# Hybrid trunk on one core: the output projection's second half in pieces, and another order of the final norm

## The chip, the cores and the metric

One core of one Trainium2 chip. The metric is the device time of one execution in microseconds, median of several runs. The core has five engines with a queue of instructions each: TensorE (PE, with its weight loads listed as PEld), VectorE (DVE), ScalarE (ACT), GpSimd (POOL) and SyncE (SP), which here only issues DMAs. Matmuls write accumulators in PSUM; a tile there that takes one bank is 128 partitions by 512 fp32 numbers.

## The reference

A trunk of two layers on x (512 positions by 1024 features, fp32), each a token mixer and a dense MLP with residual adds, and a last norm:

```python
def rmsnorm(x, g):
    y = xf * lax.rsqrt(jnp.mean(xf * xf, axis=-1, keepdims=True) + RMS_EPS)
    return (y * g).astype(x.dtype)

h = x
for layer in range(DEPTH):                       # 2
    hn = rmsnorm(h, norm_mix[layer])
    if layer % N_MIXERS == 0:                    # layer 0: 16 heads of 64, softmax over a band
        mix = chunked_band_attention(hn, attn_w_qkv[j], attn_w_o[j], attn_rel_bias[j])
    else:                                        # layer 1: gated linear recurrence
        mix = rglru_block(hn, ...)
    h = h + mix
    h = h + sq_relu_mlp(rmsnorm(h, norm_mlp[layer]), mlp_w1[layer], mlp_w2[layer])
return rmsnorm(h, norm_final)
```

The attention adds a bias to the scores by relative position, takes the softmax over each position's band of keys, weighs v by it, and multiplies the heads' outputs by w_o.

## The kernel before, in words

All activations are held transposed, features on the partitions: `hT[m]` (named h or x in the trace) is the residual of feature tile m, 128 features by 512 positions, eight tiles in all. Each fp32 product is made of two parts of each factor, a rounded high one (`hnH`, `wh`, `kh`, `pH`, `oH`) and the rest (`hnL`, `wl`, `kl`, `pL`, `oL`): `mm3` (L201 to 204) issues three matmuls, high by high, high by low and low by high. Weights come in blocks of 512 KB (`wr`, buffer pool of three, issued by SP); ACT makes `wh` of a block (L132) and DVE `wl` (L135).

**Attention.** Heads go in pairs p (heads 2p and 2p+1). For a pair the projection gives q and k; `k_out` scales k (`tk`, DVE), ACT makes `kh`, DVE `kl`, and SP copies each to the other half of the partitions by a DMA (L319 and L320), since a score matmul uses both halves. `score(h)` makes the scores of four blocks t of 128 positions, with 128(t+1) keys each, in three PSUM tiles: s0 holds t = 0 and 1, s1 t = 2, s2 t = 3; for each t first with kl, then with kh. DVE adds the bias and takes the maximum (L387), ACT the exponential, DVE scales. `turn(h)` transposes the result on PE (x, L414); ACT makes `pH` (L418) and DVE `pL` (L419) of it. `weigh(h)` multiplies by v into `oa` (L429 with pL, L430 with pH); ACT and DVE bring the halves together into `o`, and for a pair `oH` and `oL` are made. The output projection (`wo_steps`) adds, per feature tile, the products of four pairs' o with w_o: woA over pairs 0 to 3, woB over pairs 4 to 7.

The loop over i issues `score(i)`, `turn(i-1)` and `weigh(i-2)`, and between them `fill` takes pieces from a queue written out by hand (projections q, k, v, then woA and woB), as many as a credit allows, and only those whose condition holds: ("w", 15) means that `weigh(15)` has been issued. A scheduler then reorders the instructions of each engine by its own estimate of when each can start. PSUM has two pools of four banks: "mm" for projections, oa and wo, "at" for scores, transposes, sums and rows.

**Last norm.** In the last MLP the down projection of layer 1 is done in two halves of the positions, h = 0 and 1, 256 positions each. For each feature tile DVE adds the residual (L739); ACT squares it and DVE adds the square to `nf0acc` or `nf1acc` (L237, L238); in half 1 the square of the last tile is made on DVE and kept apart (`nf1sq`, L234). `sums` (L261) adds over the partitions by matmuls with ones, per 128 positions, into `nf1ss`; ACT takes the square root, DVE the reciprocal (`rt`, L265 and L266). `rstd` (L274) spreads `rt` over the partitions by a product with the identity, `nf1row`. Then DVE multiplies each tile by gain and row (`nf1o`, L731), and SP issues one DMA of 256 KB for every two tiles (L732). `finish` of half 0 stands in the order behind tile 1 of half 1.

At the start, `warm` multiplies ones by ones ten times.

Of the kernel before, what the change touches and what calls it, by code (L numbers as in the profile page):

```python
# [10 lines left out]
F32 = mybir.dt.float32  # L11
F32R = mybir.dt.float32r
AF = mybir.ActivationFunctionType
ALU = mybir.AluOpType

P = 128
# [24 lines left out]
def trunk(ctx: ExitStack, tc: tile.TileContext, xT, cols, win, wqkv, wo, rwin, rga, rgx, rwo, w1, w2, out):  # L41
# [10 lines left out]
    def mmp(name):  # L52
        return ps.tile([P, T], F32, name=name, tag="mm")

    def atp(name):
        return ps.tile([P, T], F32, name=name, tag="at")
# [144 lines left out]
    def mm3(acc, WH, WL, XH, XL, start, stop):  # L201
        PE.matmul(acc, WH, XH, start=start, stop=False)  # L202
        PE.matmul(acc, WH, XL, start=False, stop=False)  # L203
        PE.matmul(acc, WL, XH, start=False, stop=stop)  # L204
# [8 lines left out]

    LO, HI = slice(0, U), slice(U, T)


    class Norm:
        def __init__(self, name, gain, c0=0, n=T, late=False, flat=False):
            self.name, self.gain, self.acc, self.last, self.c, self.n = name, gain, None, None, slice(c0, c0 + n), n
            self.late, self.flat = late, flat  # L220
# [5 lines left out]

        def square(self, k, apart=False):
            if self.acc is None:
                self.acc = wk.tile([P, T], F32, name=f"{self.name}acc", tag="nacc")[:, : self.n]
                S.activation(self.acc, hT[k][:, self.c], AF.Square)  # L230
            else:
                sq = wk.tile([P, T], F32, name=f"{self.name}sq{k}", tag="nsq", bufs=2)[:, : self.n]
                if apart:
                    V.tensor_mul(sq, hT[k][:, self.c], hT[k][:, self.c])  # L234
                    self.last = sq
                    return
                S.activation(sq, hT[k][:, self.c], AF.Square)  # L237
                V.tensor_add(self.acc, self.acc, sq)  # L238

        def feed(self, k):  # L240
# [8 lines left out]
        def sums(self):  # L249
            nt = self.n // P  # L250
            ss = atp(f"{self.name}ss")
            if self.flat:
                PE.matmul(ss, ones, self.acc, start=True, stop=True)
                self.r = wk.tile([P, T], F32, name=f"{self.name}r", tag="nr")
                S.activation(self.r, ss, AF.Sqrt, bias=epsb, scale=1.0 / D)
                V.reciprocal(self.r, self.r)
                return
            parts = [self.acc] if self.last is None else [self.acc, self.last]
            for t in range(nt):
                for n, part in enumerate(parts):  # L260
                    PE.matmul(  # L261
                        ss[:, 2 * t : 2 * t + 2], part[:, t * P : (t + 1) * P], ones[:, 0:2],
                        start=n == 0, stop=n == len(parts) - 1,
                    )
            S.activation(rt[:, :nt], ss[:, 0 : 2 * nt : 2], AF.Sqrt, bias=epsb, scale=1.0 / D)  # L265
            V.reciprocal(rt[:, :nt], rt[:, :nt])  # L266

        def rstd(self):
            if self.flat:
                return self.r  # L270
            nt = self.n // P
            row = atp(f"{self.name}row")
            for t in range(nt):
                PE.matmul(row[:, t * P : (t + 1) * P], rt[:, t : t + 1].to_broadcast([P, P]), ident, start=True, stop=True)  # L274
            if self.last is not None:
                return row[:, : self.n]
            r = wk.tile([P, T], F32, name=f"{self.name}r", tag="nr")[:, : self.n]
            S.copy(r, row[:, : self.n])
            return r

# [3 lines left out]
    with ExitStack() as actx:  # L284
# [69 lines left out]

        def wo_steps(pairs, ncols, last):
            for u in range(D // ncols):
                WH, WL = want(1)
                for i in range(ncols // P):
                    m = u * (ncols // P) + i
                    acc = mmp(f"wo{pairs[0]}{m}")  # L360
                    c = slice(i * P, (i + 1) * P)
                    for n, p in enumerate(pairs):
                        mm3(acc, WH(n, c), WL(n, c), *oHL[p], n == 0, n == len(pairs) - 1)
                        yield 2
                    V.tensor_add(hT[m], acc, hT[m])
                    if last:
                        nm1.feed(m)

# [4 lines left out]
        def score(h):  # L373
# [6 lines left out]
            b = biases[h // 4]  # L380
            for t in range(4):
                n = (t + 1) * P
                PE.matmul(sc[t], q[h][:, t * P : n], kl[:, :n], start=True, stop=False)
                PE.matmul(sc[t], q[h][:, t * P : n], kh[:, :n], start=False, stop=True)
            for t in range(4):
# [58 lines left out]

        warm = atp("warm")
        for i in range(WARM):
            PE.matmul(warm[:, :P], ones, ones, start=True, stop=True)
        accs = [mmp(f"qk0{i}") for i in range(4)]
# [40 lines left out]

        def wo_(name, pairs, ncols, last):  # L490
            return [(name, wo_steps(pairs, ncols, last), ("w", 2 * pairs[-1] + 1))]

        queue = vv_(0) + qk(2) + qk(3) + qk(4) + vv_(1) + qk(5) + qk(6) + qk(7)
        queue += wo_("woA", (0, 1, 2, 3), U, False) + wo_("woB", (4, 5, 6, 7), U, True)
        at = {"s": -1, "w": -1}
# [44 lines left out]
    def constants(behind):  # L540
# [26 lines left out]
        V.tensor_add(cbias, cbias, cst[:, C_CB : C_CB + KT])  # L567

    PAIR = (slice(0, P), slice(P, 2 * P))

# [7 lines left out]
    def mlp(ly, norm, nxt, halves):  # L578
        with ExitStack() as mctx:
# [142 lines left out]

            def finish(nf):
                nf.sums()
                rf = nf.rstd()
                for m in range(0, KT, 2):
                    o = sr.tile([P, 1024], F32, name=f"{nf.name}o{m}", tag=("b11", "b21", "b22", "b12")[m // 2])
                    o = o[:, :T].rearrange("p (i c) -> p i c", i=2)
                    for i in range(2):
                        g = cst[:, C_FIN + m + i : C_FIN + m + i + 1]  # L730
                        V.scalar_tensor_tensor(o[:, i], hT[m + i][:, nf.c], g, rf, ALU.mult, ALU.mult)  # L731
                    nc.sync.dma_start(out[m * P : (m + 2) * P, nf.c].rearrange("(k p) c -> p k c", p=P), o)  # L732

            for h, nf in enumerate(norms):
                for m in range(KT):
                    acc = mmp(f"d{ly}7{m}{h}")[:, :U]
                    WH, WL = ws[m // 2]
                    project([acc], [PAIR[m % 2]], WH, WL, [(z[7, k][0][:, nf.c], z[7, k][1][:, nf.c]) for k in range(4)])
                    V.tensor_add(hT[m][:, nf.c], acc, hT[m][:, nf.c])  # L739
                    nf.square(m, h == 1 and m == KT - 1)  # L740
                    if h and m == 1:
                        finish(norms[0])
            finish(norms[1])

# [189 lines left out]
```

## Time and profile before

| | |
|---|---|
| median of the runs | 1082.8 us (1083.53, 1082.6, 1082.8) |
| the profiled execution | 1082.37 us, its span 1080.6 us |
| PE busy | 1069.6 us, 99% of the span |
| DVE, ACT, POOL busy | 863.5, 531.3, 9.0 us |
| DMA | 111.15 MB, mean 103 GB/s |

The span runs from the first to the last event of the engines and queues; the 1.8 us around it belong to the device time too. Busy times are sums of overlapping instructions: a matmul starts before the one ahead of it is through, so that the distance from one start to the next tells how long it holds PE, not its own duration. In the rows, "[0.90 <-DVE pL L419]" behind an instruction means that its engine stood idle for 0.90 us before it, and that DVE's instruction writing pL at line 419 ended that.

### The profile page before, as it was taken

The page shows a single profiled execution, that of the slowest core. Times are in us where ns is not written, and L with a number is a line of the kernel's source. Part 1 is how long each engine was busy: PE and PEld are TensorE (multiplying, and loading weights), DVE is VectorE, ACT ScalarE, POOL GpSimd, SP SyncE. Part 2 cuts the span into 40 slices and gives each one's busy share as a digit, 9 for nine tenths or more (in the row PEclk, how much of TensorE's full clock was granted, in tenths as well). Part 3 has the DMA queues.
Part 4 walks back from the last instruction along what each step waited for, and adds up shares of the span by engine and source line. Part 5 has one row for each costly group of instructions (what it writes and reads, how often), then busy time and mean ns, then how long its engine had stood idle before and what let it go on. Part 6 is the DMA issues. An engine that isn't in the chain of part 4 may idle for free.

```text
span 1080.6 us, 15337 instructions
## 1 busy us (share of the span) xinstructions
PE 1069.6 (99%) x6046; PEld 935.6 (87%) x6046; DVE 863.5 (80%) x1286; ACT 531.3 (49%) x775; POOL 9.0 (1%) x28
## 2 busy tenths in 40 slices
PE   9999999999999999999999999999999999999996
PEld 7888888888899999898988888888889999989896
DVE  6889788879887787776777989879887777787665
ACT  6667567565443343342444688366443343343321
POOL 0010000000000000000000000000000000000000
PEclk9999999999999999999999999999999999999999
DMA  8354253341432323322232222442431432332102
GB/s 275 98 140 134 59 176 98 83 152 59 137 117 79 117 89 107 99 81 96 76 122 77 78 64 73 151 142 68 147 117 59 136 98 79 117 94 83 59 1 79
DMA packets 112919, 111.15 MB, mean 103 GB/s; under 512 B 4176, under 2 KB 106704, under 8 KB 112848
## 3 DMA queue, kind: packets, MB, share of 16 engines
q1 hardware_dynamic: 112560, 109.99, 33.1%
q8 instruction: 47, 0.77, 0.3%
q14 instruction: 24, 0.20, 0.1%
q10 hardware_dynamic: 288, 0.20, 0.1%
HBM read 103.87 MB, written 2.10 MB: 98 GB/s over the span
## 4 chain that ended last, share of the span: by engine, by line
PE 96%; DVE 2%; ACT 1%; DMA 1%; issue 0%; SPq 0%; DVEq 0%; ACTq 0%
PE d L203 11%; PE d L202 11%; PE d L204 11%; PE p L204 9%; PE p L203 9%; PE p L202 9%; PE x L414 1%; PE wo L203 1%; PE wo L202 1%; PE ro L202 1%; PE v L202 1%; PE ro L204 1%; PE v L204 1%; PE wo L204 1%; PE xb L202 1%; PE xb L204 1%
## 5 line engine op out<-in xcount | busy, mean ns | idle before, releaser
L132 ACT CAST wh<-wr 128x1024 fp32r<-128x1024 f32 (+1 forms) x129 | 133.6, 1039 | 201.6 <-PE d L203 88.8
L203 PE MATMUL d<-zL,wh 128*128 128x512 f32 (+1 forms) x544 | 206.3, 379 | 0.0
L202 PE MATMUL d<-zH,wh 128*128 128x512 f32 (+1 forms) x544 | 205.1, 379 | 0.0
L204 PE MATMUL d<-zH,wl 128*128 128x512 f32 (+1 forms) x544 | 204.8, 377 | 0.0
L132 ACT CAST wh<-b 128x1024 fp32r<-128x1024 f32 x98 | 101.3, 1047 | 174.8 <-PE p L203 76.0
L135 DVE TENSOR_TENSOR wl<-wr,wh 128x1024 fp32r<-128x1024 f32 (+1 forms) x130 | 156.2, 1203 | 23.3 <-ACT wh L132 23.1
L135 DVE TENSOR_TENSOR wl<-b,wh 128x1024 fp32r<-128x1024 f32 x98 | 118.7, 1219 | 42.9 <-ACT wh L132 42.8
L204 PE MATMUL p<-tH,wl 128*128 128x256 f32 x448 | 126.8, 283 | 0.0
L203 PE MATMUL p<-tL,wh 128*128 128x256 f32 x448 | 126.8, 283 | 0.0
L202 PE MATMUL p<-tH,wh 128*128 128x256 f32 x448 | 126.6, 282 | 0.0
L204 PEld LDWEIGHTS d<-zH,wl 128*128 128x128 f32 x544 | 102.4, 188 | 19.1
L202 PEld LDWEIGHTS d<-zH,wh 128*128 128x128 f32 x544 | 102.5, 189 | 16.8
L203 PEld LDWEIGHTS d<-zL,wh 128*128 128x128 f32 x544 | 102.7, 189 | 16.3 <-DVE zL L623 0.5
L678 DVE TENSOR_TENSOR h<-d,h 128x512 f32<-128x512 f32 x120 | 82.2, 686 | 38.9 <-PE d L204 38.3
L204 PE MATMUL p<-hnH,wl 128*128 128x256 f32 x336 | 95.1, 283 | 0.0
L203 PE MATMUL p<-hnL,wh 128*128 128x256 f32 x336 | 95.1, 283 | 0.0
L202 PE MATMUL p<-hnH,wh 128*128 128x256 f32 x336 | 94.9, 282 | 0.0
L202 PEld LDWEIGHTS p<-tH,wh 128*128 128x128 f32 x448 | 85.8, 192 | 1.6
L203 PEld LDWEIGHTS p<-tL,wh 128*128 128x128 f32 x448 | 85.8, 192 | 1.6
L204 PEld LDWEIGHTS p<-tH,wl 128*128 128x128 f32 x448 | 85.8, 192 | 0.0
L202 PEld LDWEIGHTS p<-hnH,wh 128*128 128x128 f32 x336 | 64.3, 191 | 1.7
L203 PEld LDWEIGHTS p<-hnL,wh 128*128 128x128 f32 x336 | 64.3, 191 | 1.6
(336 smaller groups left out, 2071.6 us busy)
## 6 DMA issues: line engine op xcount, KB each, us to landing
wr<-in_w SPq DMA_DIRECT2D x72, 512.0 KB, 3.5
b<-in_w SPq DMA_DIRECT2D x56, 512.0 KB, 4.4
wr<-in_wqkv SPq DMA_DIRECT2D x20, 512.0 KB, 4.0
wr<-in_rwin SPq DMA_DIRECT2D x16, 512.0 KB, 3.6
wr<-in_wo SPq DMA_DIRECT2D x8, 512.0 KB, 4.2
wr<-in_rwo SPq DMA_DIRECT2D x8, 512.0 KB, 3.4
x<-in_xT SPq DMA_DIRECT2D x8, 256.0 KB, 4.3
bias<-in_win SPq DMA_DIRECT2D x4, 512.0 KB, 4.5
```

Source lines behind the costliest of these rows:

```text
L132: S.copy(H[:, :n], raw[:, :n])
L135: low = V.tensor_sub(L[:, :n], raw[:, :n], f(H[:, :n]))
L202: PE.matmul(acc, WH, XH, start=start, stop=False)
L203: PE.matmul(acc, WH, XL, start=False, stop=False)
L204: PE.matmul(acc, WL, XH, start=False, stop=stop)
L414: PE.transpose(b[:, c : c + P], pt[:, seg[t] + kt * P : seg[t] + (kt + 1) * P], ident)
L678: V.tensor_add(hT[m], acc, hT[m])
```

## The change

It has three parts.

1. `wo_steps` takes a range of weight blocks. Block 0 of woB is split: `wo_open` multiplies pairs 4, 5 and 6 for its two feature tiles as soon as `weigh(13)` is issued, `wo_close` adds pair 7 after `weigh(15)`; the other blocks follow as before.
2. `score` goes through the blocks t in the order 3 and 2, 0, 1, and for each of these first with kh, then with kl.
3. In the last norm, ACT multiplies each tile by its gain as soon as the tile is there (`scale`, into the output tiles). What is left, the product with the row, is done on DVE for four tiles at once (128x1024) and one DMA of 512 KB. In half 1 the squares of tiles 6 (ACT) and 7 (DVE) are kept apart, the two sums have a bank each and a square root each, five products on ones by ones (`idle`) are written ahead of the last sums and of the row, and the row is made twice: DVE takes the one in PSUM for tiles 0 to 3 and then 4 and 5, ACT copies the other for GpSimd, which does tiles 6 and 7 and whose DMA ACT issues. The outputs of half 1 go in DMAs of 512, 256 and 256 KB.

`warm` is now written with `idle` and takes its bank from the "mm" pool.

```diff
+    PAIR = (slice(0, P), slice(P, 2 * P))
+    def idle(n):
+        bank = mmp("idle")
+        for _ in range(n):
+            PE.matmul(bank[:, :P], ones, ones, start=True, stop=True)
...
-        def square(self, k, apart=False):
+        def square(self, k, apart=None):
             if self.acc is None:
                 self.acc = wk.tile([P, T], F32, name=f"{self.name}acc", tag="nacc")[:, : self.n]
                 S.activation(self.acc, hT[k][:, self.c], AF.Square)
+                self.parts.append(self.acc)
+                return
+            sq = wk.tile([P, T], F32, name=f"{self.name}sq{k}", tag="nsq", bufs=2)[:, : self.n]
+            if apart is V:
+                V.tensor_mul(sq, hT[k][:, self.c], hT[k][:, self.c])
             else:
-                sq = wk.tile([P, T], F32, name=f"{self.name}sq{k}", tag="nsq", bufs=2)[:, : self.n]
-                if apart:
-                    V.tensor_mul(sq, hT[k][:, self.c], hT[k][:, self.c])
-                    self.last = sq
-                    return
                 S.activation(sq, hT[k][:, self.c], AF.Square)
+            if apart is None:
                 V.tensor_add(self.acc, self.acc, sq)
+            else:
+                self.parts.append(sq)
...
-            parts = [self.acc] if self.last is None else [self.acc, self.last]
-            for t in range(nt):
-                for n, part in enumerate(parts):
+            if len(self.parts) > 1:
+                ss = [atp(f"{self.name}ss{t}")[:, 0:2] for t in range(nt)]
+            else:
+                row = atp(f"{self.name}ss")
+                ss = [row[:, 2 * t : 2 * t + 2] for t in range(nt)]
+            for n, part in enumerate(self.parts):
+                if n and n == len(self.parts) - 1:
+                    idle(2)
+                for t in range(nt):
                     PE.matmul(
-                        ss[:, 2 * t : 2 * t + 2], part[:, t * P : (t + 1) * P], ones[:, 0:2],
-                        start=n == 0, stop=n == len(parts) - 1,
+                        ss[t], part[:, t * P : (t + 1) * P], ones[:, 0:2],
+                        start=n == 0, stop=n == len(self.parts) - 1,
                     )
-            S.activation(rt[:, :nt], ss[:, 0 : 2 * nt : 2], AF.Sqrt, bias=epsb, scale=1.0 / D)
+            if len(self.parts) > 1:
+                for t in range(nt):
+                    S.activation(rt[:, t : t + 1], ss[t][:, 0:1], AF.Sqrt, bias=epsb, scale=1.0 / D)
+            else:
+                S.activation(rt[:, :nt], row[:, 0 : 2 * nt : 2], AF.Sqrt, bias=epsb, scale=1.0 / D)
             V.reciprocal(rt[:, :nt], rt[:, :nt])
 
-        def rstd(self):
+        def rstd(self, copies=1):
             if self.flat:
                 return self.r
             nt = self.n // P
-            row = atp(f"{self.name}row")
-            for t in range(nt):
-                PE.matmul(row[:, t * P : (t + 1) * P], rt[:, t : t + 1].to_broadcast([P, P]), ident, start=True, stop=True)
-            if self.last is not None:
-                return row[:, : self.n]
+            rows = [atp(f"{self.name}row{i}") for i in range(copies)]
+            if copies > 1:
+                idle(3)
+            for row in rows:
+                for t in range(nt):
+                    PE.matmul(row[:, t * P : (t + 1) * P], rt[:, t : t + 1].to_broadcast([P, P]), ident, start=True, stop=True)
             r = wk.tile([P, T], F32, name=f"{self.name}r", tag="nr")[:, : self.n]
-            S.copy(r, row[:, : self.n])
-            return r
+            S.copy(r, rows[-1][:, : self.n])
+            return r if copies == 1 else (r, rows[0][:, : self.n])
...
+        open_ = []
+        def wo_tile(m, acc, last):
+            V.tensor_add(hT[m], acc, hT[m])
+            if last:
+                nm1.feed(m)
+        def wo_steps(pairs, us, last):
+            for u in us:
                 WH, WL = want(1)
-                for i in range(ncols // P):
-                    m = u * (ncols // P) + i
-                    acc = mmp(f"wo{pairs[0]}{m}")
-                    c = slice(i * P, (i + 1) * P)
+                for i in range(2):
+                    acc = mmp(f"wo{pairs[0]}{2 * u + i}")
                     for n, p in enumerate(pairs):
-                        mm3(acc, WH(n, c), WL(n, c), *oHL[p], n == 0, n == len(pairs) - 1)
+                        mm3(acc, WH(n, PAIR[i]), WL(n, PAIR[i]), *oHL[p], n == 0, n == len(pairs) - 1)
                         yield 2
-                    V.tensor_add(hT[m], acc, hT[m])
-                    if last:
-                        nm1.feed(m)
+                    wo_tile(2 * u + i, acc, last)
+        def wo_open(pairs):
+            WH, WL = want(1)
+            accs = [mmp(f"wo{pairs[0]}{i}") for i in range(2)]
+            open_.extend((WH, WL, accs))
+            for n, p in enumerate(pairs[:-1]):
+                for i in range(2):
+                    mm3(accs[i], WH(n, PAIR[i]), WL(n, PAIR[i]), *oHL[p], n == 0, False)
+                    yield 2
+        def wo_close(pairs):
+            WH, WL, accs = open_
+            n = len(pairs) - 1
+            for i in range(2):
+                mm3(accs[i], WH(n, PAIR[i]), WL(n, PAIR[i]), *oHL[pairs[-1]], False, True)
+                wo_tile(i, accs[i], True)
+                yield 2
 
         seg = [0, P, 3 * P, 6 * P]
...
-            for t in range(4):
-                n = (t + 1) * P
-                PE.matmul(sc[t], q[h][:, t * P : n], kl[:, :n], start=True, stop=False)
-                PE.matmul(sc[t], q[h][:, t * P : n], kh[:, :n], start=False, stop=True)
+            for ts in ((3, 2), (0,), (1,)):
+                for n, (kx, first) in enumerate(((kh, True), (kl, False))):
+                    for t in ts:
+                        PE.matmul(sc[t], q[h][:, t * P : (t + 1) * P], kx[:, : (t + 1) * P], start=first, stop=not first)
...
-        def wo_(name, pairs, ncols, last):
-            return [(name, wo_steps(pairs, ncols, last), ("w", 2 * pairs[-1] + 1))]
+        A, B = (0, 1, 2, 3), (4, 5, 6, 7)
         queue = vv_(0) + qk(2) + qk(3) + qk(4) + vv_(1) + qk(5) + qk(6) + qk(7)
-        queue += wo_("woA", (0, 1, 2, 3), U, False) + wo_("woB", (4, 5, 6, 7), U, True)
+        queue += [("woA", wo_steps(A, range(4), False), ("w", 7)), ("wo0", wo_open(B), ("w", 13))]
+        queue += [("wo1", wo_close(B), ("w", 15)), ("woB", wo_steps(B, range(1, 4), True), ("w", 15))]
...
+            scaled = {}
+            def scale(h, nf, m):
+                if m % 4 == 0:
+                    scaled[h, m // 4] = sr.tile([P, 1024], F32, name=f"nf{h}o{m}", tag=("b11", "b21", "b22", "b12")[2 * h + m // 4])
+                o = scaled[h, m // 4].rearrange("p (i c) -> p i c", i=4)
+                S.activation(o[:, m % 4], hT[m][:, nf.c], AF.Copy, scale=cst[:, C_FIN + m : C_FIN + m + 1])
+            def finish(h, nf):
                 nf.sums()
-                rf = nf.rstd()
-                for m in range(0, KT, 2):
-                    o = sr.tile([P, 1024], F32, name=f"{nf.name}o{m}", tag=("b11", "b21", "b22", "b12")[m // 2])
-                    o = o[:, :T].rearrange("p (i c) -> p i c", i=2)
-                    for i in range(2):
-                        g = cst[:, C_FIN + m + i : C_FIN + m + i + 1]
-                        V.scalar_tensor_tensor(o[:, i], hT[m + i][:, nf.c], g, rf, ALU.mult, ALU.mult)
-                    nc.sync.dma_start(out[m * P : (m + 2) * P, nf.c].rearrange("(k p) c -> p k c", p=P), o)
+                cuts = ((0, 4, V, nc.sync), (4, 4, V, nc.sync))
+                if h == 0:
+                    by = {V: nf.rstd()}
+                else:
+                    cuts = ((0, 4, V, nc.sync), (6, 2, G, nc.scalar), (4, 2, V, nc.sync))
+                    by = dict(zip((G, V), nf.rstd(2)))
+                for m, n, eng, queue in cuts:
+                    o = scaled[h, m // 4].rearrange("p (i c) -> p i c", i=4)[:, m % 4 : m % 4 + n]
+                    eng.tensor_mul(o, o, by[eng][:, None, :].to_broadcast([P, n, U]))
+                    queue.dma_start(out[m * P : (m + n) * P, nf.c].rearrange("(k p) c -> p k c", p=P), o)
 
             for h, nf in enumerate(norms):
                 for m in range(KT):
@@ -737,10 +789,11 @@
                     WH, WL = ws[m // 2]
                     project([acc], [PAIR[m % 2]], WH, WL, [(z[7, k][0][:, nf.c], z[7, k][1][:, nf.c]) for k in range(4)])
                     V.tensor_add(hT[m][:, nf.c], acc, hT[m][:, nf.c])
-                    nf.square(m, h == 1 and m == KT - 1)
+                    nf.square(m, {KT - 2: S, KT - 1: V}.get(m) if h else None)
+                    scale(h, nf, m)
                     if h and m == 1:
-                        finish(norms[0])
-            finish(norms[1])
+                        finish(0, norms[0])
+            finish(1, norms[1])
```

The scheduler places these instructions anew. PE's order between head 14's oa (oa_2381) and head 15's (oa_2394 before, oa_2420 now); oH_1813, oH_2067, oH_2356 are pairs 4, 5, 6, wo_2400 and wo_2401 the two opened tiles. Before:

```order
L429 MATMUL oa_2381<-pL_2265,v_1270 128x256
L430 MATMUL oa_2381<-pH_2264,v_1270 128x256 [waits Activation_49]
L429 MATMUL oa_2381<-pL_2265,v_1270 128x128
L430 MATMUL oa_2381<-pH_2264,v_1270 128x128
L429 MATMUL oa_2394<-pL_2374,v_1270 128x512 [waits DVE_49]
L430 MATMUL oa_2394<-pH_2373,v_1270 128x512 [waits Activation_49]
L202 MATMUL wo_2416<-oH_1813,wh_2125 128x512
L429 MATMUL oa_2394<-pL_2374,v_1270 128x384 [waits DVE_49]
```

Now (the rows left out are of wo_2400 and wo_2401 too):

```order
L475 MATMUL oa_2381<-pL_2265,v_1270 128x128
L476 MATMUL oa_2381<-pH_2264,v_1270 128x128
L202 MATMUL wo_2400<-oH_1813,wh_2125 128x512 [waits DVE_49]
L203 MATMUL wo_2400<-oL_1814,wh_2125 128x512
...
L202 MATMUL wo_2401<-oH_2356,wh_2125 128x512
L203 MATMUL wo_2401<-oL_2357,wh_2125 128x512
L204 MATMUL wo_2401<-oH_2356,wl_2126 128x512
L475 MATMUL oa_2420<-pL_2374,v_1270 128x512 [waits PE_49]
L476 MATMUL oa_2420<-pH_2373,v_1270 128x512
```

Head 15's first oa stood right behind head 14's last; now 18 wo matmuls stand between them.

SP's order of DMAs at pair 7, whose copies are kh_2085 and kl_2086 (head 14), kh_2091 and kl_2092 (head 15); wr_2312 is a 512 KB block of w_o. Before:

```order
L319 DMA kh_2085<-kh_2085 64x512 [waits DMAHW0_49,PE_49,Activation_49]
L319 DMA kh_2091<-kh_2091 64x512 [waits DMAHW1_49,PE_49,Activation_49]
L320 DMA kl_2086<-kl_2086 64x512 [waits DMAHW2_49,DVE_49]
L320 DMA kl_2092<-kl_2092 64x512 [waits DMAHW3_49,DVE_49]
L117 DMA wr_2312<-in_wo 128x4x256 [waits DMAHW4_49]
L117 DMA wr_2412<-in_w 128x4x256 [waits DMAHW6_49,DMAHW5_49,DVE_49]
```

Now:

```order
L343 DMA kh_2085<-kh_2085 64x512 [waits DMAHW0_49,PE_49,Activation_49]
L343 DMA kh_2091<-kh_2091 64x512 [waits DMAHW1_49,PE_49,Activation_49]
L117 DMA wr_2312<-in_wo 128x4x256 [waits DMAHW2_49,DVE_49]
L344 DMA kl_2086<-kl_2086 64x512 [waits DMAHW3_49,DVE_49]
L344 DMA kl_2092<-kl_2092 64x512 [waits DMAHW4_49,DVE_49,PE_49]
L117 DMA wr_2396<-in_w 128x4x256 [waits DMAHW6_49,DMAHW5_49,DVE_49]
```

wr_2312 has moved from behind the copies of kl to ahead of them, and with it a wait for DVE.

PE's last rows: d_9927 before and d_9933 now are the last down projection, nf1sq_9930 and nf1sq_9947 the squares of tiles 6 and 7. Before:

```order
L204 MATMUL d_9927<-zH_9615,wl_9535 128x256
L261 MATMUL nf1ss<-ones,nf1acc 128x2 [waits DVE_49]
L261 MATMUL nf1ss<-ones,nf1sq_9941 128x2 [waits DVE_49]
L261 MATMUL nf1ss<-ones,nf1acc 128x2
L261 MATMUL nf1ss<-ones,nf1sq_9941 128x2
L274 MATMUL nf1row<-ident,rt 128x128 [waits DVE_49]
L274 MATMUL nf1row<-ident,rt 128x128
```

Now:

```order
L204 MATMUL d_9933<-zH_9615,wl_9535 128x256
L279 MATMUL nf1ss_9950<-ones,nf1acc 128x2 [waits DVE_49]
L279 MATMUL nf1ss_9951<-ones,nf1acc 128x2
L279 MATMUL nf1ss_9950<-ones,nf1sq_9930 128x2 [waits Activation_49]
L279 MATMUL nf1ss_9951<-ones,nf1sq_9930 128x2
L221 MATMUL idle<-ones 128x128 x5
L279 MATMUL nf1ss_9950<-ones,nf1sq_9947 128x2 [waits DVE_49]
L279 MATMUL nf1ss_9951<-ones,nf1sq_9947 128x2
L300 MATMUL nf1row_9964<-ident,rt 128x128 [waits DVE_49]
L300 MATMUL nf1row_9964<-ident,rt 128x128 [waits Activation_49]
L300 MATMUL nf1row_9965<-ident,rt 128x128 [waits PE_49]
```

The five products on ones, written two ahead of the last sums and three ahead of the row, now stand together ahead of the last sums, and the row is there twice.

More of the change, by code (lines that the diff above doesn't have):

```diff
@@ L214, in trunk @@
     LO, HI = slice(0, U), slice(U, T)
+    PAIR = (slice(0, P), slice(P, 2 * P))
[3 more added lines that the diff above has]
+            PE.matmul(bank[:, :P], ones, ones, start=True, stop=True)
     class Norm:
         def __init__(self, name, gain, c0=0, n=T, late=False, flat=False):
-            self.name, self.gain, self.acc, self.last, self.c, self.n = name, gain, None, None, slice(c0, c0 + n), n
+            self.name, self.gain, self.acc, self.parts, self.c, self.n = name, gain, None, [], slice(c0, c0 + n), n
             self.late, self.flat = late, flat
@@ L250, in sums @@
             nt = self.n // P
-            ss = atp(f"{self.name}ss")
             if self.flat:
+                ss = atp(f"{self.name}ss")
                 PE.matmul(ss, ones, self.acc, start=True, stop=True)
@@ L353, in v_steps @@
                         )
-        def wo_steps(pairs, ncols, last):
-            for u in range(D // ncols):
+        open_ = []
[5 more added lines that the diff above has]
+            for u in us:
                 WH, WL = want(1)
-                for i in range(ncols // P):
-                    m = u * (ncols // P) + i
-                    acc = mmp(f"wo{pairs[0]}{m}")
-                    c = slice(i * P, (i + 1) * P)
+                for i in range(2):
+                    acc = mmp(f"wo{pairs[0]}{2 * u + i}")
                     for n, p in enumerate(pairs):
-                        mm3(acc, WH(n, c), WL(n, c), *oHL[p], n == 0, n == len(pairs) - 1)
+                        mm3(acc, WH(n, PAIR[i]), WL(n, PAIR[i]), *oHL[p], n == 0, n == len(pairs) - 1)
                         yield 2
-                    V.tensor_add(hT[m], acc, hT[m])
-                    if last:
-                        nm1.feed(m)
+                    wo_tile(2 * u + i, acc, last)
[14 more added lines that the diff above has]
+                yield 2
         seg = [0, P, 3 * P, 6 * P]
@@ L442, in weigh @@
                 oHL[p] = (oH, oL)
-        warm = atp("warm")
-        for i in range(WARM):
-            PE.matmul(warm[:, :P], ones, ones, start=True, stop=True)
+        idle(WARM)
         accs = [mmp(f"qk0{i}") for i in range(4)]
@@ L567, in constants @@
         V.tensor_add(cbias, cbias, cst[:, C_CB : C_CB + KT])
-    PAIR = (slice(0, P), slice(P, 2 * P))
     def mlp(ly, norm, nxt, halves):
@@ L721, in mlp @@
             norms = [Norm(f"nf{h}", C_FIN, h * U, U) for h in range(2)]
-            def finish(nf):
-                nf.sums()
-                rf = nf.rstd()
-                for m in range(0, KT, 2):
-                    o = sr.tile([P, 1024], F32, name=f"{nf.name}o{m}", tag=("b11", "b21", "b22", "b12")[m // 2])
-                    o = o[:, :T].rearrange("p (i c) -> p i c", i=2)
-                    for i in range(2):
-                        g = cst[:, C_FIN + m + i : C_FIN + m + i + 1]
-                        V.scalar_tensor_tensor(o[:, i], hT[m + i][:, nf.c], g, rf, ALU.mult, ALU.mult)
-                    nc.sync.dma_start(out[m * P : (m + 2) * P, nf.c].rearrange("(k p) c -> p k c", p=P), o)
+            scaled = {}
[5 more added lines that the diff above has]
+            def finish(h, nf):
+                nf.sums()
+                cuts = ((0, 4, V, nc.sync), (4, 4, V, nc.sync))
[8 more added lines that the diff above has]
+                    queue.dma_start(out[m * P : (m + n) * P, nf.c].rearrange("(k p) c -> p k c", p=P), o)
             for h, nf in enumerate(norms):
```

## The prediction

> **What bounds the kernel now.** I read the page first, then windows along the span, PE's waits, and the timelines of the places where PE waits. The page's first line has the busy shares of the engines; the second quoted line has the shares of the chain that ended last.
>
> ```profile
> PE 1069.6 (99%) x6046; PEld 935.6 (87%) x6046; DVE 863.5 (80%) x1286; ACT 531.3 (49%) x775; POOL 9.0 (1%) x28
> ...
> PE 96%; DVE 2%; ACT 1%; DMA 1%; issue 0%; SPq 0%; DVEq 0%; ACTq 0%
> ```
>
> TensorE is the bound. The change takes no matmul out; it adds seven (five products on ones, two for the second row). So the time can move only where PE has gaps: in the attention, and in the tail behind the last matmul. Windows (first columns: the stretch, its length, PE's busy time), then PE's waits from 40 to 230 us:
>
> ```profile
> 216.00:225.00 9.00, 8.10 (x48) 7.15 (x47) 5.42 (x8) 5.83 (x10) 0.00 (x0) 1.00 0.34 108
> 225.00:1060.00 835.00, 834.88 (x4820) 737.07 (x4820) 665.40 (x820) 381.10 (x446) 0.00 (x0) 1.00 0.30 95
> ```
> ```profile
> PE oa L429 <- DVE pL L419: 0.9, 1, 0.9
> PE s L383 <- DMA kl<-kl: 0.3, 1, 0.3
> ```
>
> 835 us of MLP and recurrent layer hold 0.12 us of idle PE and PE's order there is the same: I cost that stretch at nothing. In the attention 1.2 us of waits show. Some hide under overlapping matmuls, as in these scores of head 15, 128x256 and then 128x384:
>
> ```profile
> 200.56 0.28 PE L384 MATMUL s<-kh,q 128*128 128x256 f32 x1
> 200.89 0.44 PE L383 MATMUL s<-kl,q 128*128 128x384 f32 x1
> ```
>
> The 128x256 one holds PE for .33 us; behind the same instruction of head 14 the next started after .12 (197.95 and 198.07, quoted below). The .21 is a wait for the bank's last reader. With, as an estimate, such lags at five to eight heads, all that the attention could give back is 1.2 + 1.0 to 1.7, or 2.2 to 2.9 us.
>
> **Part 1, the output projection opened early.** The one large wait is oa of head 15, whose pL comes late:
>
> ```profile
> 221.10 0.28 PE L430 MATMUL oa<-pH,v 128*128 128x128 f32 x1
> 222.28 0.50 PE L429 MATMUL oa<-pL,v 128*128 128x512 f32 x1 [0.90 <-DVE pL L419]
> 222.62 0.39 PE L430 MATMUL oa<-pH,v 128*128 128x512 f32 x1
> 222.85 0.39 PE L202 MATMUL wo<-oH,wh 128*128 128x512 f32 x1
> ```
>
> From 221.10 to 222.28 PE issues one matmul of 128 columns, which elsewhere takes about .11 (128x256: .12 above): 1.07 us lost. A 512-wide matmul takes .23 (222.62 to 222.85). The order now puts 18 of them, ready early, between oa of head 14 and oa of head 15: 18 x .23 = 4.1 us, four times the wait. So **-1.1**. Is something else late next? Behind oa of head 15, oH and oL of pair 7 have to be made:
>
> ```profile
> 224.41 0.28 PE L430 MATMUL oa<-pH,v 128*128 128x128 f32 x1
> ...
> 226.07 0.62 ACT L440 CAST oH<-o 128x512 fp32r<-128x512 f32 x1 [0.76 <-DVE o L436]
> ...
> 226.72 0.69 DVE L441 TENSOR_TENSOR oL<-o,oH 128x512 fp32r<-128x512 f32 x1 [0.69 <-ACT oH L440]
> ```
>
> oH is done 2.28 us after that matmul started, oL 3.00. Now ten wo matmuls stand behind it: .11 + 10 x .23 = 2.4 until oH is wanted, and three more, 3.1, until oL is. It just fits: 0, at most +.3.
>
> **Part 2, the scores' order.** kh now comes first, and the tiles in the order 3, 2, 0, 1. The scheduler moves the rest along: first heads of pairs go ahead on PE, and on SP's queue at pair 7 the 512 KB weight block for wo is put between kh's copies and kl's. SP's, DVE's and PE's rows there, and the latency of kl's copies:
>
> ```profile
> 193.47 1.11 SPq L319 DMA_DIRECT2D kh<-kh  x2
> 194.67 1.20 SPq L320 DMA_DIRECT2D kl<-kl  x2
> 195.92 0.58 SPq L117 DMA_DIRECT2D wr<-in_wo  x1
> ```
> ```profile
> DMA to landing us min/median/max: 2.2/2.3/4.7
> ```
> ```profile
> 191.51 0.68 DVE L441 TENSOR_TENSOR oL<-o,oH 128x512 fp32r<-128x512 f32 x1
> ...
> 192.71 1.22 DVE L135 TENSOR_TENSOR wl<-wr,wh 128x1024 fp32r<-128x1024 f32 x1
> ```
> ```profile
> 194.46 0.40 PE L429 MATMUL oa<-pL,v 128*128 128x512 f32 x1
> 194.70 0.39 PE L430 MATMUL oa<-pH,v 128*128 128x512 f32 x1
> ...
> 197.38 0.40 PE L203 MATMUL wo<-oL,wh 128*128 128x512 f32 x1
> 197.61 0.22 PE L383 MATMUL s<-kl,q 128*128 128x128 f32 x1
> ...
> 197.95 0.28 PE L384 MATMUL s<-kh,q 128*128 128x256 f32 x1
> 198.07 0.34 PE L383 MATMUL s<-kl,q 128*128 128x384 f32 x1
> ```
>
> Before, PE reached head 14's scores at 197.61 and did not wait (.23 behind the matmul ahead). Now the first score with kh stands behind one oa matmul, at 194.70. kh's copy, issued at 193.47 as now, would land at 193.47 + 2.3 = 195.8: a wait of up to 1.1. DVE makes tk ahead of oL (.68 sooner) but behind two other 64x512 subtractions that it used to do earlier, so kh may be issued .5 earlier or some tenths later; I take .6 lost. Behind it stand some 2.7 us of matmuls (oa's remainder, three scores, transposes, two of wo), so PE wants kl at 194.70 + 2.7 = 197.4, or 198.0 with that wait. wr can be issued when wl is made (192.71 + 1.22 = 193.93), takes .58, and kl follows at 194.7 or later. On SP's queue kl is issued about as before; what is new is 512 KB ahead of it. The longest landing of kl, 4.7, is the nearest row for that, 2.3 the other end. So kl lands between 197.0 and 199.4: a wait of 0 to 2.0 (with the kh wait not counted twice); I take 199.4 less 198.0 = 1.4, since the latency view has such a case. Together **+2.0**, bounds 0 and 2.6.
>
> The second heads ask first for the banks that are freed last (tile 3's). A bank wait cost .21 above; with one more such wait at each of five heads the cost is 1.0, with all of the old ones gone the gain is as much. I take **+.2**. Head 4's .3 stays: kh is now what it waits for.
>
> **Part 3, the tail.** PE's rows, DVE's, ACT's and SP's:
>
> ```profile
> 1070.28 0.28 PE L204 MATMUL d<-zH,wl 128*128 128x256 f32 x1
> ...
> 1071.69 0.38 PE L261 MATMUL nf1ss<-ones,nf1sq 128*128 128x2 f32 x2 [0.41 <-DVE nf1sq L234]
> 1071.93 0.36 PE L261 MATMUL nf1ss<-ones,nf1acc 128*128 128x2 f32 x2
> 1072.15 0.36 PE L261 MATMUL nf1ss<-ones,nf1sq 128*128 128x2 f32 x2
> 1073.07 0.71 PE L274 MATMUL nf1row<-ident,rt 128*128 128x128 f32 x4 [0.55 <-DVE rt L266]
> ```
> ```profile
> 1072.85 0.17 DVE L266 RECIPROCAL rt<-rt 128x2 f32<-128x2 f32 x1 [1.22 <-ACT rt L265]
> 1073.82 3.22 DVE L731 SCALAR_TENSOR_TENSOR nf1o<-h,cst,nf1row 128x256 f32<-128x256 f32 x8 [0.81 <-PE nf1row L274]
> ```
> ```profile
> 1074.72 2.72 SPq L732 DMA_DIRECT2D out<-nf1o  x4
> ```
> ```profile
> GB/s 0 0 0 0 0 0 156 333 319 326 350 317 352 101 0 0 0 0 0 0 0 0 0 0 0 0 0 0 0 233 313 344 324 339 337 333 51 0 0 0
> ```
>
> The last line (slices of .465 us from 1062) says what the end hangs on: once the first output starts, about 1 us behind its issue at 1074.72, 1.05 MB flow at some 335 GB/s without a gap, 3.2 us. Only when the first issue comes counts, not how fast DVE makes the rest. So weights multiplied ahead, which cut DVE's 3.22 us, and the GpSimd share gain nothing unless they bring that first issue forward. They put it back:
> - Now the five products on ones stand together ahead of the last two sums. Four fp32 matmuls of 128 took .71 here, so with .36 for the last one a pitch of about .117, two to a product: five products take 1.1 to 1.2. They start when the four sums before them are through. The last d matmul starts at 1070.28 and the first sum at about 1070.40; with .23 a sum (1071.93 to 1072.15) the ones run from 1071.3 to 1072.4. Without them the last sums could start by 1071.69, when the square was there before; now it comes a little sooner, since one addition ahead of it is gone. The last of the two sums starts at 1072.64 instead of 1072.15, so reciprocal and row are **+.48** late.
> - The first DMA now needs one 128x1024 product, about 1.22 (as wl's) instead of two of 3.22/8 = .40: 1.22 - .87 (1073.82 to the issue, less the queue's .03) gives **+.35**.
>
> Together +.8. Range: if the ones slip into waits, -.2; if ACT's two square roots and the 512 KB transfer each start later, +1.2.
>
> GpSimd does tiles 6 and 7, 128x512 with two inputs, hidden while it ends before the stream wants it: 768 KB are ahead of it, 2.3 us, so about 2.6 us are free. Its nearest rows:
>
> ```profile
> 22.61 1.42 POOL L295 COPY bias<-bias 128x256 f32<-128x256 f32 x4 [21.13 <-DMA bias<-in_win]
> ...
> 71.11 2.69 POOL L295 COPY bias<-bias 128x256 f32<-128x256 f32 x4 [46.83 <-DMA bias<-in_win]
> ```
>
> .35 to .67 a copy; double the columns, double the inputs: 1.4 to 2.7. I take 1.4 and nothing on the path. The ones also serve no clock:
>
> ```profile
> 1070.00:1074.00 4.00, 2.48 (x17) 1.91 (x15) 1.53 (x5) 0.64 (x2) 0.00 (x0) 1.00 0.00 0
> 1074.00:1080.60 6.60, 0.00 (x0) 0.00 (x0) 3.04 (x8) 0.00 (x0) 0.00 (x0) 0.63 0.49 160
> ```
>
> the granted clock is 1.00 through the row. [...]
>
> **Sum.** -1.1 + 2.0 + .2 + .8 = +1.9 on the profiled run's 1082.37 (span 1080.6 and 1.8 around it): 1084.3. That run lies .4 under the median of the runs, 1082.8, within their spread of .9. A measurement of this kernel can tell 0.2%, 2.2 us, so below 1080.6 is faster and above 1085.0 slower.
>
> **Rivals.**
> - Slower, by kl alone: the weight block holds kl back by its whole transfer and kh too is late. Price 1.1 + 2.6 = 3.7 at head 14, sum +3.6: 1086.0. It decides once kl lands after about 199.7. For it: the 4.7 landing; against: the median of 2.3. Chance .20.
> - Faster: kl and kh are in time, since DVE makes tk sooner, and bank waits go as well: -1.1 - 1.0 + .8 = -1.3, 1081.1; with the ones in the waits down to 1080.1. For it: 2.2 to 2.9 us of waits are there; against: the order of SP's queue. Chance .22.
> [...]
> - No effect from the opening: oa of head 15 still waits, for a bank or oL of pair 7: +3.0, 1085.4. Chance .05.
>
> My forecast has the other .48.
>
> **Chances.** Faster by over 0.2%: a third of the faster rival, .08. Slower: most of kl's rival (.18), GpSimd's .05, the fourth's .03 and a fifth of the forecast, .10: .36. Within: .56. The range reaches from the faster rival, 1081.0, to a little above kl's, 1086.6.
>
> **What would show it.** Right: no wait of PE for pL at 222; a wait of PE for the DMA of kh or kl at 195 to 199, 1 to 2.5 us; the ones in one block at 1071.3, the row at 1073.5, the first output issue at 1075.5; the end 4.8 us or more behind the row. Wrong: PE without a wait at head 14, the first output issue before 1075, a POOL product over 2.6 us.

## The result, and the profile after

The changed kernel took 1084.57 us in the median of 22 runs (1083.51 to 1087.49), the kernel before 1082.82 us on the same chips (22 runs, 1082.38 to 1084.54). The ratio is 1.0016 with a 95% interval of [1.001, 1.0023]: slower by 1.75 us, inside the bound of 0.2% that the prediction called no change, but a real loss. The forecast was 1084.3.

The span of the profiled run is 1083.3 us instead of 1080.6. The distance between the same instructions of the two traces tells where the time went. Each number is the changed kernel's time less that of the kernel before:

| up to | late by, us |
|---|---|
| first score matmul (40.3 before) | +0.32 |
| last matmul of pair 7's k (188.6) | +2.07 |
| last matmul of wo (245.7) | +2.05 |
| last down projection (1070.3) | +1.75 |
| first row matmul (1073.1) | +2.14 |
| end of the span (1080.6) | +2.75 |

So the attention lost 1.73 us net of its start, the stretch behind it gave 0.30 back, and the tail lost 1.00 in this pair of runs. The starts of PE's matmuls, with the usual distance from one to the next taken off, show nearly all of the 1.73. Lost are .92 at head 1 (a wait for DVE's v that comes and goes with the same code, see the last section), .36 ahead of a transpose at 164, .76 at head 12 and 1.20 at head 14. Gained are 1.07 at head 15's oa and .47 at head 4, where kl was waited for. Together that is 1.70.

PE's waits from 40 to 230 us in the changed kernel:

```profile
PE s L430 <- DVE v L374: 0.8, 1, 0.8
PE s L430 <- DMA kh<-kh: 0.6, 1, 0.6
PE s L430 <- DMA kl<-kl: 0.5, 1, 0.5
PE x L460 <- DVE pL L465: 0.4, 1, 0.4
PE x L460 <- DVE p L447: 0.2, 1, 0.2
```

The 0.9 for oa behind pL is gone. PE's rows there show head 15's oa following at the usual distance, with no idle time named:

```profile
228.17 0.39 PE L203 MATMUL wo<-oL,wh 128*128 128x512 f32 x1
228.40 0.39 PE L204 MATMUL wo<-oH,wl 128*128 128x512 f32 x1
228.63 0.39 PE L475 MATMUL oa<-pL,v 128*128 128x512 f32 x1
228.86 0.39 PE L476 MATMUL oa<-pH,v 128*128 128x512 f32 x1
```

New are the waits of score matmuls for DMAs. At head 12 it is kh (first fence), at head 14 kl (second), where SP now issues wo's block between the copies (third; the fourth is the latency of kl's copies, minimum, median and maximum):

```profile
176.61 0.39 PE L204 MATMUL qk7q_out<-hnH,wl 128*128 128x512 f32 x1
177.60 0.70 PE L430 MATMUL s<-kh,q 128*128 128x512 f32 x3 [0.61 <-DMA kh<-kh]
```
```profile
196.53 0.39 PE L475 MATMUL oa<-pL,v 128*128 128x512 f32 x1
196.76 0.63 PE L430 MATMUL s<-kh,q 128*128 128x512 f32 x3
...
198.96 0.40 PE L203 MATMUL wo<-oL,wh 128*128 128x512 f32 x1
199.73 0.44 PE L460 MATMUL x<-ident,p 128*128 128x128 f32 x2 [0.37 <-DVE pL L465]
200.66 0.74 PE L430 MATMUL s<-kl,q 128*128 128x512 f32 x3 [0.50 <-DMA kl<-kl]
```
```profile
194.25 1.11 SPq L343 DMA_DIRECT2D kh<-kh  x2
195.45 0.54 SPq L117 DMA_DIRECT2D wr<-in_wo  x1
196.08 1.15 SPq L344 DMA_DIRECT2D kl<-kl  x2
```
```profile
DMA to landing us min/median/max: 2.2/2.3/5.6
```

Starts tell more than the idle times: 177.60 follows 176.61 by .99 where .23 is usual, .76 lost; at head 14 the x at 199.73 comes .54 late, and kl's score, .93 behind it, about .66 late. kl's copy was issued at 196.08 and its score started at 200.66, 4.6 us behind.

The tail, in the rows of PE, DVE, GpSimd and SP:

```profile
1072.03 0.28 PE L204 MATMUL d<-zH,wl 128*128 128x256 f32 x1
1072.15 0.50 PE L279 MATMUL nf1ss<-ones,nf1acc 128*128 128x2 f32 x4
1072.51 0.59 PE L279 MATMUL nf1ss<-ones,nf1sq 128*128 128x2 f32 x4
1072.96 1.36 PE L221 MATMUL idle<-ones 128*128 128x128 f32 x10
1074.16 0.51 PE L279 MATMUL nf1ss<-ones,nf1sq 128*128 128x2 f32 x4
1075.21 1.16 PE L300 MATMUL nf1row<-ident,rt 128*128 128x128 f32 x8 [0.55 <-DVE rt L288]
```
```profile
1072.81 0.42 DVE L243 TENSOR_TENSOR nf1sq<-h 128x256 f32<-128x256 f32 x1
1074.99 0.17 DVE L288 RECIPROCAL rt<-rt 128x2 f32<-128x2 f32 x1 [1.76 <-ACT rt L285]
1075.96 1.82 DVE L783 TENSOR_TENSOR nf1o<-nf1o,nf1row 128x1024 f32<-128x1024 f32 x2 [0.80 <-PE nf1row L300]
```
```profile
1076.86 1.27 POOL L783 TENSOR_TENSOR nf1o<-nf1o,nf1r 128x512 f32<-128x512 f32 x1 [907.28 <-ACT nf1r L302]
```
```profile
1077.26 0.99 SPq L784 DMA_DIRECT2D out<-nf1o  x2
```

The square of the last tile is done at 1073.23, and the last sums could start then; the ones hold PE from 1072.96 to 1074.16, 1.20 us. From the last down projection to the row it is 3.18 us instead of 2.79, from there to the first output's issue 2.05 instead of 1.65: together +.79.

### The profile page after: what moved, and what is told of

The parts are those of the page before. It is cut to its first block, busy times and chain, and to the rows that moved or that the text cites. A ratio compares the mean times of both kernels' runs of the same rounds, so it can differ in the third digit from the quotient of the medians.

```text
span 1083.3 us, 15366 instructions
## 1 busy us (share of the span) xinstructions
PE 1072.1 (99%) x6064; PEld 937.6 (87%) x6064; DVE 860.7 (79%) x1273; ACT 538.8 (50%) x793; POOL 10.8 (1%) x29
## 4 chain that ended last, share of the span: by engine, by line
PE 85%; issue 7%; DVE 4%; DMA 2%; ACT 2%; POOLq 0%; SPq 0%; ACTq 0%; DVEq 0%
PE d L202 9%; PE d L203 9%; PE d L204 9%; PE p L204 8%; PE p L203 8%; PE p L202 8%; PE s L430 2%; PE x L460 1%; PE ro L202 1%; PE ro L204 1%; DMA wr<-in_wqkv 1%; PE xb L202 1%; PE xb L204 1%; PE u L204 1%; PE u L202 1%
```

## Experiments: which part costs what

All are compared with the kernel before, 1082.8 to 1082.9 in each group of runs.

**The parts alone.** The kernel before with only the opening (it and the next one have the changed kernel's `warm`):

```diff
-queue += wo_("woA", ...) + wo_("woB", (4, 5, 6, 7), U, True)
+queue += [("woA", wo_steps(A, range(4), False), ("w", 7)), ("wo0", wo_open(B), ("w", 13))]
+queue += [("wo1", wo_close(B), ("w", 15)), ("woB", wo_steps(B, range(1, 4), True), ("w", 15))]
```

> The kernel before with only the first block of woB opened early (scores and tail as before). Theory A (the three parts add up: opening -1.1, score order about +2.5, tail about +0.9): 1.1 us under before, about 1081.7, and no wait of PE for pL near 222. Rival B (the opening moves the wait to oH and oL of pair 7, and the tail carries the whole loss): as before, 1082.8, with a new wait of 1 us behind head 15's oa.

Measured: 1081.75, ratio 0.9989 [0.998, 0.9998], -1.1 us. PE has no wait left from 205 to 230 us:

```profile
216.00:225.00 9.00, 9.00 (x51) 7.83 (x50) 6.02 (x9) 4.08 (x7) 0.00 (x0) 1.00 0.37 117
```

PE is busy for all of the nine microseconds in which it lacked .90 before. A holds, B falls.

The kernel before with only the scores' order:

```diff
-for t in range(4):
-    n = (t + 1) * P
-    PE.matmul(sc[t], q[h][:, t * P : n], kl[:, :n], start=True, stop=False)
-    PE.matmul(sc[t], q[h][:, t * P : n], kh[:, :n], start=False, stop=True)
+for ts in ((3, 2), (0,), (1,)):
+    for n, (kx, first) in enumerate(((kh, True), (kl, False))):
+        for t in ts: ...
```

> The kernel before with only the scores' order (3 and 2, 0, 1; kh ahead of kl). Theory A: 2 to 3 us over before, about 1085.3: PE waits at head 1, 12 and 14 as in the changed kernel, and the wait for pL near 222 is still there. Rival B: within 0.5 us of before, 1082.8, since the waits at heads 12 and 14 take place of others that go.

Measured: 1086.69 (7 runs, 1084.87 to 1089.94), ratio 1.0039 [1.0025, 1.0052], +3.8. The profiled run, at 1085.36 among the shorter ones, has PE waiting for kh twice (0.9 the longest), for kl, and for pL as before:

```profile
PE s L413 <- DMA kh<-kh: 1.1, 2, 0.9
PE oa L458 <- DVE pL L448: 0.9, 1, 0.9
PE s L413 <- DMA kl<-kl: 0.4, 1, 0.4
```

A is right in kind; the median is above its range, and the runs scatter over 5 us, which neither theory had. The scatter goes with the granted clock, given as a mean over the span: the three shortest runs, 1084.87 to 1085.36, are where A has them and show .997 or .998, the four from 1086.69 up show .994 to .996. A clock lower by .004 over 1085 us is some 4 us, an estimate from these figures. So part of the +3.8 may be the clock's and not the order's.

The changed kernel with the tail of before, and the changed kernel with the scores of before:

```diff
# oldtail: class Norm and finish() as before; opening and score order stay
# oldscores: for t in range(4): kl, then kh, as before; opening and tail stay
```

> The changed kernel with the tail of before (opening and score order stay). Theory A: 0.9 us under the changed kernel, about 1083.7. Rival B (the tail carries all of the 1.75 us): 1082.8.

> The changed kernel with the scores' order of before (opening and new tail stay). Theory A: -1.1 for the opening and +0.9 for the tail, 1082.6, and on SP's queue the weight block of w_o behind kl's copies again. Rival B: 1084.5, as the changed kernel.

Measured: 1084.33 with the old tail, ratio 1.0012 [1.0003, 1.0021]; 1081.97 with the old scores, 0.9994 [0.9985, 1.0002]. So the scores' order costs 2.6 us in the changed kernel (1084.57 - 1081.97; 1084.33 - 1081.75 in the pair with the old tail gives 2.6 too). The new tail costs only .2 in the medians (1084.57 - 1084.33, and 1081.97 - 1081.75), not the .8 forecast. By the scatter of the runs .2 is little more than nothing. The old tail's profile has something that the profile before did not have:

```profile
1073.06 1.22 PE L281 MATMUL nf1row<-ident,rt 128*128 128x128 f32 x4 [0.55 <-DVE rt L273]
```
```profile
1072.00:1073.00 1.00, 0.50 (x5) 0.41 (x4) 0.17 (x1) 0.26 (x1) 0.00 (x0) 0.99 0.00 0
1073.00:1074.00 1.00, 0.94 (x4) 0.93 (x4) 0.00 (x0) 0.00 (x0) 0.00 (x0) 0.50 0.00 0
```

The same four row matmuls took 1.22 us instead of .71, since the granted clock (third column from the right) was .50 by then.

**Which half of the scores' order.** One kernel keeps kh ahead but goes through the blocks as before, the other keeps the new blocks but puts kl ahead:

```diff
# khfirst
-for ts in ((3, 2), (0,), (1,)):
+for ts in ((0,), (1,), (2,), (3,)):
# order32
-enumerate(((kh, True), (kl, False)))
+enumerate(((kl, True), (kh, False)))
```

> The changed kernel with the blocks of the scores in the order 0, 1, 2, 3 as before, but kh still ahead of kl. Theory A (kh ahead lets the scheduler put first heads earlier on PE than their copies land, and kl behind the weight block; the order of the blocks matters little): within 0.5 us of the changed kernel, 1084.1 to 1085, with waits for kh at head 12 and for kl at head 14. Rival B (the order of the blocks, which asks for the bank freed last, costs the time): 1082.5 or less.

> The changed kernel with the blocks in the new order 3, 2, 0, 1, but kl ahead of kh as before. Theory A: 1082.2 to 1083, near the kernel with the scores of before (1082.0), since PE comes to head 14 about 3 us later than with kh ahead; the weight block still stands ahead of kl on SP's queue, which then no longer shows as 1.2 us of waits. Rival B: 1084.5, as the changed kernel.

Measured: 1084.75, ratio 1.0017 [1.0008, 1.0026], with kh ahead; 1082.24, 0.9992 [0.9983, 1.0001], with kl ahead. A holds: it is kh ahead that costs 2.5 us (1084.75 - 1082.24), the order of the blocks .3 at most (1082.24 against 1081.97). With kh ahead the waits are the DMAs' again:

```profile
PE s L430 <- DMA kl<-kl: 1.2, 1, 1.2
PE s L430 <- DMA kh<-kh: 1.1, 2, 0.9
```

**What kh ahead does.** It draws the scores forward on PE. The weight block then stands ahead of kl, but that is not kh's doing alone: the kernel with kl ahead and the new order of the blocks has it there too, and waits for kl:

```profile
193.48 1.11 SPq L343 DMA_DIRECT2D kh<-kh  x2
194.68 0.54 SPq L117 DMA_DIRECT2D wr<-in_wo  x1
195.31 1.15 SPq L344 DMA_DIRECT2D kl<-kl  x2
```
```profile
PE s L430 <- DMA kl<-kl: 0.4, 1, 0.4
```

It takes 1082.24 all the same. Its kl score at head 14 starts 4.4 us behind the copy's issue (199.70), nearly as late as in the changed kernel, but PE comes there late enough to lose only .4 to .6. So the block's place costs much only together with scores that are drawn forward. The next kernel keeps kh ahead and undoes the block's place: the last block of w_o is issued behind pair 7's kl.

```diff
-nc.sync.dma_start(f(kl[oth]), f(kl[own]))
+state['kl'] = nc.sync.dma_start(f(kl[oth]), f(kl[own]))
...
+if starts and i == starts[0] - 1:
+    after(load, state['kl'])
```

> The changed kernel with one more order: the last weight block of w_o goes on SP's queue behind kl's copies of pair 7, where it was before the change. The scheduler then also puts the scores with kl of head 14 some 2 us earlier on PE. Theory A1 (the weight block ahead of kl makes kl late): the waits of 1.2 us ahead of head 14's kl scores (0.54 and 0.66) go, 1083.5. Theory A2 (kh ahead draws the scores too far forward whatever stands on SP's queue): a wait for kl stays, 1084.3 or more.

Measured: 1082.83, ratio 0.9999 [0.999, 1.0008], 1.7 us under the changed kernel. SP's rows now have kl ahead, and among PE's waits that for kl is gone while kh's stays:

```profile
193.52 1.11 SPq L345 DMA_DIRECT2D kh<-kh  x2
195.20 1.22 SPq L346 DMA_DIRECT2D kl<-kl  x2
196.47 0.59 SPq L117 DMA_DIRECT2D wr<-in_wo  x1
```
```profile
PE s L432 <- DMA kh<-kh: 0.8, 2, 0.5
PE x L462 <- DVE mx L435: 0.3, 1, 0.3
PE x L462 <- DVE p L449: 0.2, 1, 0.2
```

A1 holds: with kh ahead, one 512 KB load ahead of two copies of some 2.3 us costs up to 1.7 us, two thirds of what the scores' order loses. The edit also let the scheduler put head 14's kl scores earlier, so the 1.7 is the queue's order with what the scheduler makes of it. The two profiles show less than 1.7 of it at the place itself: what is lost at head 14 falls from 1.20 to .42, and another .6 is head 1's wait for v, which is smaller in this run. That kernel is level with the kernel before; the waits for kh, .8, are about what stays.

**The tail.** Both kernels start from the one with the scores of before, 1081.97, whose runs scatter little. The first has no products on ones; the second multiplies and sends tiles 0 and 1 first:

```diff
# noones
-if n and n == len(self.parts) - 1:
-    idle(2)
-if copies > 1:
-    idle(3)
# smallfirst
-cuts = ((0, 4, V, nc.sync), (6, 2, G, nc.scalar), (4, 2, V, nc.sync))
+cuts = ((0, 2, V, nc.sync), (2, 2, V, nc.sync), (6, 2, G, nc.scalar), (4, 2, V, nc.sync))
```

> The kernel with the scores of before (1082.0), and without the five products on ones. Theory A (they only hold the last sums up by 0.5 us; the clock holds through the row in most runs): row 2.75 us behind the last down projection instead of 3.18, time 1081.5. Rival C (without them the granted clock falls ahead of the row in most runs, as in the run with the old tail, where the four row matmuls took 1.22 us instead of 0.71): 1082.0 or more, and a row at half the clock.

> The kernel with the scores of before (1082.0), with tiles 0 and 1 multiplied and sent ahead of tiles 2 and 3 (128x512 and 256 KB each, instead of 128x1024 and 512 KB). Theory A (the end hangs on the first output's issue): the first issue 0.5 us earlier and the time 0.5 less, 1081.5. Rival D (the end hangs on when the last piece is issued, or on the products): 1082.0.

Measured: 1081.22, ratio 0.9984 [0.9975, 0.9993], without the ones, and 1081.10, 0.9981 [0.9972, 0.9991], with the small first piece: .75 and .87 under their base. A holds for both, and for the small piece the gain is more than A's .5. Without the ones the last sums wait .19 for the square and the row follows the last down projection by 2.41 us instead of 3.18. With the small piece the row starts as in the base (1072.41 and 1072.40), and the first issue comes at 1073.92 instead of 1074.45; that is .53 of the gain, and the rest is a shorter way from there to the end (5.33 for 5.74), whose cause is open:

```profile
1070.51 0.61 PE L277 MATMUL nf1ss<-ones,nf1sq 128*128 128x2 f32 x4 [0.19 <-DVE nf1sq L243]
1071.66 1.16 PE L296 MATMUL nf1row<-ident,rt 128*128 128x128 f32 x8 [0.55 <-DVE rt L286]
```
```profile
1073.92 1.58 SPq L784 DMA_DIRECT2D out<-nf1o  x3
```

**Both, and GpSimd's share.** The best kernel so far has the opening, the scores of before, the new tail without ones and with the small first piece; beside it, the same with tiles 6 and 7 on DVE.

```diff
# best: both edits above; bestvec also:
-(6, 2, G, nc.scalar), (4, 2, V, nc.sync))
+(4, 2, V, nc.sync), (6, 2, V, nc.sync))
```

> Early opening, scores of before, new tail without the products on ones and with tiles 0 and 1 sent first: if the gains of the two tail edits add (0.75 and 0.87 under the kernel with the scores of before, 1081.97), 1080.4. Rival (both act through the same first issue and the end then hangs on GpSimd's piece): 1081.0.

> The same as the kernel sent with it (early opening, scores of before, no ones, tiles 0 and 1 first), but tiles 6 and 7 are multiplied on DVE behind tiles 4 and 5 and sent by SP; the second row is still made and copied. If the outputs' stream sets the end, no difference (within 0.2 us). If GpSimd's share brings something, 0.3 to 0.7 us slower; if GpSimd's piece is what comes last, faster.

Measured: 1080.62, ratio 0.9978 [0.9969, 0.9987], 2.2 us under the kernel before and 4 under the changed one, so that the two gains nearly add (1080.4 was forecast for that); 1081.40, 0.9986 [0.9977, 0.9995], with DVE doing all. The .8 between them can't be put down to GpSimd's share by these runs: in the second one's profile the granted clock had fallen to .50 again, and its eight row matmuls took 2.07 us instead of 1.16, so that the first issue came .5 late for that reason. That profile is of the longest of its eleven runs, 1082.42.

```profile
1072.10 2.07 PE L296 MATMUL nf1row<-ident,rt 128*128 128x128 f32 x8 [0.55 <-DVE rt L286]
```

From first issue to end it took 5.83 there and 5.34 in the best kernel, but over the eleven experiments and the two kernels this distance lies between 5.3 and 6.2 with no clear order (5.9 to 6.1 in the four with the old tail, 5.4 to 6.2 in the five with the new tail as it was changed), so the rest stays open.

## Why the prediction held, and where it did not

The total was right (1084.3 for 1084.57). The signs of all three parts were right, but that the total came so close is in part luck: the scores cost .4 more than the sum had and the tail .6 less.

- **Opening, -1.1.** Right: -1.13 alone, the wait for pL gone, and no wait for oH or oL of pair 7 in its place. The cover of 18 matmuls was ample: head 15's oa came at 228.63 with no idle time.
- **The stretch behind, 0.** Slightly off, and its premise wrong: the prediction said that PE's order there is the same, but the opening also reorders some matmuls of the first MLP. From that MLP's first product p (268.62 us before) to the last down projection the changed kernel takes .34 us less (801.32 for 801.66), and the kernel with the opening alone .36 less. The count of seven added matmuls is two short, since the sums of tile 6's square are new too; the sum for the tail has them in its "four sums before them", so no term hangs on it.
- **Scores, +2.2** (2.0 for head 14, .2 for bank waits at second heads). Right in mechanism, a little small: 2.6 in the medians. Of the parts, kl behind the weight block was well placed: 4.6 us from issue to use, for a forecast of 4.7, and undoing it gave 1.7 back, for 1.4. The trace has less at head 14 than the 2.0: 1.20, of which .66 is kl and .54 a transpose that waits for pL. The .6 for kh was put at the wrong head. At head 14 nothing waited for kh, because PE came there at 196.76, not 194.70; it waited at head 12, .76, for which the sum had no term. The order of the blocks, where the prediction suspected the bank freed last, cost .3 at most.
- **Tail, +.8.** This is the step that failed, in its size. Its parts were found as forecast in the trace: row +.39 (for .48), from the row to the first issue +.40 (for .35). The medians gave +.2. Two things were not in the sum. First, the sum was made against a profile in which the clock held through the row; it does not always. Of seven profiles without the ones (before, openonly, scoreonly, oldtail, noones, best, bestvec) two had the row at a granted clock of .50 (1.22 us for .71, and 2.07 for 1.16), +.5 each; of the six with them none. Second, the end follows the first issue less closely than I had it, 5.3 to 6.2 us behind it. That these two make up the whole difference between .8 and .2 is argued, not shown.
- **"The ones also serve no clock".** Wrong as it stands. One profile, in which the granted clock was 1.00 through the row, can't carry it: in the old tail's run the clock fell to .50 at about 1073.0, 2.4 us behind the end of the last down projection, with sums between and no gap of PE over .55. Still, on balance, the ones lost: removing them gained .75, since they stood in the path and not in the waits.
- **GpSimd.** 1.27 us, for 1.4 forecast, and it started .08 behind the copy that it waited for (ACT's copy ran from 1076.41, .37 long). With the scores of before, without the ones, with the small piece and in the best kernel it is 1.26 or 1.27 too. The chances have .05 for GpSimd as the cause of a slower kernel; no run shows the product above 2.6 us that this would need.

The faster rival, in which kl and kh are in time, did not come about: PE waited for both. Nor did the slower one, in which head 14 alone costs 3.7: the trace has 1.20 lost there.

## What to carry to other kernels

Read a scheduler's new order on every queue, the DMA queue too: an edit to matmuls moved a 512 KB load ahead of two small copies and brought PE to them sooner, and putting the load back behind them won 1.7 us. Where PE came to them later, the same load ahead cost .4 to .6. Where an output stream flows without a gap once it has begun, as here (331 and 343 GB/s from 1079 to 1081 us in the changed kernel), the time of the first issue is what counts: send a small piece first (.87 us here), and let no filler stand ahead of the chain that leads to it (.75). A term worked out from one profile is one draw where the clock may fall in between; ask what the row would cost at half the clock (here 1.22 us for .71).

## What the runs showed that I had not expected

The granted clock can fall during the sparse matmuls of the tail at different times from run to run: by 1073.0 in one run with the old tail, .1 us before the row, and in the profile before only about 1.9 us behind the row's end. The price is .5 us for four fp32 row matmuls (1.22 for .71).

Nine of the profiles show when it falls, by the granted clock of a window that is 1.00 before and .50 behind it. In two (old tail, DVE doing all) it falls within .1 us of the row's start; with the opening alone .1 us behind the row's end; and 1.0 to 2.7 us behind the row's end in the other six (before, changed, scores' order alone, scores of before, without the ones, small first piece). What makes it fall sooner in one run than in another stays open: the opening alone and the old tail have the same tail, and their falls come .8 us behind the row's start and .1 ahead of it. Whether the ones kept the clock in their six profiles was not tested.

Head 1's first scores wait .3 to .8 us for DVE's v in eight of the thirteen profiles and not at all in the lists of the other five. It is .8 with the opening alone, none with the scores' order alone, and .5 and none in the last two kernels, whose attention is the same. So this wait, .8 in the list of the changed kernel's waits, comes and goes with the same code and can't be put down to the change.

The kernel with the scores' order alone scattered over 5 us (1084.87 to 1089.94), where the kernel before scattered over 2. Its longer runs had less of the clock (.994 to .996, for .997 and .998); why they had is open, since only one of the short ones was profiled.
